# Scaling attention probabilities on GpSimd or ScalarE only, and adding FoX's causal mask in PSUM

## The chip, the cores and the metric

One core of a Trainium2 chip runs the whole program in one launch. The metric is device microseconds of one execution, and of several executions the median. The engines are TensorE (PE, with its weight loads as PEld), VectorE (DVE), ScalarE (ACT), GpSimd (POOL) and SyncE, whose queue (SP) issues every DMA.

## The reference

A decoder trunk of two residual layers over 512 tokens of width 1024, all in float32. Layer 0 mixes with DSA (kind "a": an indexer picks the top 128 keys, the rest is masked) and with FoX (kind "b": causal attention with a forgetting bias), eight heads of 64 each. Layer 1 mixes with NSA: sixteen heads, each with a compressed, a selected and a window branch that are merged by sigmoid gates. Each layer ends with a squared-ReLU MLP of width 4096. What the change touches is the softmax:

```python
def masked_softmax(s, mask):
    s = jnp.where(mask, s.astype(jnp.float32), -jnp.inf)
    m = jnp.max(s, axis=-1, keepdims=True)
    e = jnp.where(mask, jnp.exp(s - m), 0.0)
    return e / jnp.maximum(jnp.sum(e, axis=-1, keepdims=True), 1e-30)

# FoX, per block of 128 queries
logits = (q @ k.T) * scale + cum_q - cum_k            # cum: running sum of log-forget gates
p = masked_softmax(logits, key_pos <= t)
# NSA, merge
out = g0 * o_compressed + g1 * o_selected + g2 * o_window
```

## The kernel before

Every dense product is done with float32r matmuls of a high and a low part, three for one (`mm3`): weights arrive in `raw` tiles of 128x512, ScalarE (or VectorE) rounds the high part into `whi`, VectorE or GpSimd forms the low part `wlo`. In the MLP seven products of a Strassen scheme take the place of eight (`psm`).

The order of the work on each engine isn't written by hand. Generators yield operations, or lists of alternatives on different engines, and a planner (`Planner`) simulates the machine when the kernel is built: it takes the operation that can start first by its cost table (`_price`) and its latencies (`LATENCY`, `MARGIN`), breaks ties by priority (attention 10, evacuations 12, top-k 16, weights 18), and picks the alternative with the earliest end. VectorE's costs are raised by up to four times with its recent load (`BIAS`), GpSimd's and ScalarE's are not. The order is then fixed: each engine works through its list, and waits where an operand isn't there yet. Changed prices or alternatives therefore reorder the list of every engine.

Attention is done in units: one head and one block of 128 queries `qb` against n = 128 (qb + 1) keys (`unit`, line 770). A unit takes a tile `t` (four exist), forms the bias, runs two matmuls into a PSUM bank `pss` (two exist), adds the bias and takes the row extreme in one VectorE operation (`nm`), runs Exp on ScalarE with the row sum `den`, the reciprocal `rec` on VectorE, scales the probabilities by `rec` and, in NSA, by the gate (`gat`), transposes them on TensorE by the identity (`ptp`, two banks) and copies them out to `pt`, from which the products with the values are run (`po`). The scaling is one operation with two factors, on GpSimd or VectorE:

```python
        g = 1.0 if gate is None else gate
        yield [e.tensor_scalar(t[:, :n], t[:, :n], rec, g, op0=OP.mult, op1=OP.mult) for e in (G, V)]
```

There are 64 units in layer 0 (32 FoX units first, then 32 DSA units, whose bias `scr` is the finished top-k mask) and 128 in layer 1 (selected and window branch; the bias is the causal mask alone). Only a FoX unit forms its bias: `b_bias` (line 1152) adds the broadcast row of the head's cumulated gates (`bb`, two tiles, brought by a DMA) and the causal mask (`cm`, a part of the constants tile `call`) into `t`, on VectorE or GpSimd. Up to six units run beside each other (`WIN`), and between them dense matmuls of the same layer.

`ident` and `cm` lie in `call`, which comes in one DMA, issued by `load_thread` (line 456) ahead of the fifth weight tile. The identity is used by every transpose, and for the diagonal matrices `dg` in `Stats.end` (line 606), by which the row norms are turned at the start.

Of the kernel before, what the change touches and what calls it, by code (L numbers as in the profile page):

```python
# [9 lines left out]
F32R = mybir.dt.float32r  # L10
AF = mybir.ActivationFunctionType
OP = mybir.AluOpType
AX = mybir.AxisListType.X

P = 128
S = 512
# [1 line left out]
NEG = -1e30  # L18
GONE = -3e38
EPS = 1e-6  # L20
CONSTS = [("gains", 32), ("ident", 128), ("cm", 512), ("kvg", 2), ("kig", 1), ("bfg", 1), ("rowv", 1),
          ("pek", 16), ("pev", 16), ("bgate", 48), ("cmm", 128), ("w2k", 128), ("w2v", 64),
          ("fold", 62)]
CONST_AT, NCONST = {}, 0
for _n, _w in CONSTS:
    CONST_AT[_n] = (NCONST, _w)
# [21 lines left out]
PR_ATT = 10  # L48
PR_EV = 12
# [119 lines left out]
class Planner:  # L169
# [16 lines left out]
    def spawn(self, gen, prio):  # L186
        self.count += 1
        self.resume([gen, prio, 0.0, None, self.count], None)
# [8 lines left out]
    def put(self, slots, *tiles):  # L197
        for t in tiles:
            slots.free.append((self.now, self.engine))
            slots.back(t)  # L200
        self.serve()
# [76 lines left out]
    def bias(self, engine, t):  # L278
        b = BIAS.get(engine, 0)
        if not b:  # L280
            return 0
        last, load = self.load.get(engine, (0.0, 0.0))
        load *= math.exp(-max(0.0, t - last) / TAU)
        return b * max(0.0, load - FLOOR)
# [58 lines left out]
def group(ops):  # L343
    o = Op(ops[0].engine, 0.0, [], [], [])
    for x in ops:
        o.cost += x.cost
        o.calls += x.calls
        o.reads += x.reads
        o.writes += x.writes
    return o  # L350
# [3 lines left out]
def trunk(ctx: ExitStack, tc: tile.TileContext, A):  # L354
# [3 lines left out]
    def pool(name, bufs, space=bass.MemoryType.SB):  # L358
        return ctx.enter_context(tc.tile_pool(name=name, bufs=bufs, space=space))

    cp, sp, mp, few, xq = pool("cp", 1), pool("sp", 1), pool("mp", 24), pool("few", 4), pool("xq", 1)
# [6 lines left out]
    K = Slots(pool("kp", 8), "k", 8, full, F32R)  # L368
    Q = Slots(pool("qp", 8), "q", 8, full, F32R)
    TU = Slots(pool("tu", N_TU), "tu", N_TU, full)  # L370
    TE = Slots(pool("te", N_TE), "te", N_TE, full)
# [11 lines left out]
    V, SC, G, T = (Queue(n, e) for n, e in  # L383
                   (("DVE", nc.vector), ("ACT", nc.scalar), ("POOL", nc.gpsimd), ("PE", nc.tensor)))
    SY = Queue("SP", nc.sync)
    spawn, put, done = pl.spawn, pl.put, pl.set
# [4 lines left out]
    def small(n, name="sm"):  # L391
        return mp.tile([P, n], F32, tag=f"m{n}", name=name)

    def copy(out, src):
        return [SC.activation(out, src, AF.Copy), V.tensor_copy(out, src)]
# [27 lines left out]
    mhalf = cp.tile([P, 4], F32, name="mhalf")  # L423
    C = {n: call[:, o:o + w] for n, (o, w) in CONST_AT.items()}
    gains = gall.rearrange("p (a k) -> p a k", k=KT)
    ident, cm = C["ident"], C["cm"]
    cmm = C["cmm"].rearrange("p (a b) -> p a b", b=32)
    rowv, kvg, bgate = C["rowv"], C["kvg"], C["bgate"]
    bfg, kig = C["bfg"][0:8], C["kig"][0:64]
# [18 lines left out]
    def shaped(t, shape):  # L448
# [4 lines left out]
            return t[:, :n].rearrange("p (a b) -> p a b", b=shape[1])  # L453
        return t[:, :n]

    def load_thread():
        yield SY.dma_start(gall, A["consts"][:, 0:32])
        at = 0
        for j in jobs:
            if j.load is not None:  # L460
                yield from j.load()
            for i, (src, shape) in enumerate(j.chunks):
                n = shape[0] * shape[1]
                if at in X_AT:
                    for k in range(*X_AT[at]):
                        x = yield O.get("x", F32)
                        yield SY.dma_start(x, A["xT"][:, k, :])
                        done(x0[k], x)
                if at in XN_AT:
                    done(xnf[XN_AT.index(at)])  # L470
                if at == CONST_PUT:
                    yield SY.dma_start(call, A["consts"])
                at += 1
                raw = yield RAW.get("raw")
                yield SY.dma_start(raw[:, :n], src)
                done(j.raw[i], raw)
# [277 lines left out]
        return (yield ("all", [slots.get(name, dtype), slots.get(name, dtype)]))  # L754


    def scores(ps, qs, kk, qb):
        n = P * (qb + 1)
        q = qs[:, qb * P:(qb + 1) * P]
        return group([T.matmul(ps[:, :n], q, kk[0][:, :n], start=True, stop=False),  # L760
                      T.matmul(ps[:, :n], q, kk[1][:, :n], start=False, stop=True)])

    def pt_dst(pt, h, qb):
        if h == 0:
            return pt[:, 0:qb + 1, qb * P:(qb + 1) * P]
        base = pt[:, 4 - qb, 0:P]
        return bass.AP(tensor=base.tensor, offset=base.offset,
                       ap=[base.ap[0], [S + P, qb + 1], [1, P]])

    def unit(qs, kk, qb, bias, pt, h, fut, gate=None):  # L770
        n = P * (qb + 1)
        t = yield TU.get("t")
        b = yield from bias(t)
        ps = yield PSS.get("pss")
        yield scores(ps, qs, kk, qb)
        nm, den, rec = small(1, "nm"), small(1, "den"), small(1, "rec")
        yield V.tensor_tensor_reduce(out=t[:, :n], in0=ps[:, :n], in1=b, op0=OP.add, op1=OP.min,
                                     scale=-0.125, scalar=3e38, accum_out=nm)
        put(PSS, ps)
        yield SC.activation(t[:, :n], t[:, :n], AF.Exp, scale=-1.0, bias=nm, accum_out=den)  # L780
        yield V.reciprocal(rec, den)
        g = 1.0 if gate is None else gate
        yield [e.tensor_scalar(t[:, :n], t[:, :n], rec, g, op0=OP.mult, op1=OP.mult) for e in (G, V)]
        tt = yield PST.get("ptp")
        yield group([T.transpose(tt[:, j * P:(j + 1) * P], t[:, kb * P:(kb + 1) * P], ident)
                     for kb in range(qb + 1) for j in [kb if h == 0 else qb - kb]])
        put(TU, t)
        yield copy(pt_dst(pt, h, qb), tt[:, :n].rearrange("p (a b) -> p a b", b=P))
        put(PST, tt)
        done(fut)  # L790
# [138 lines left out]
    used = {h: 0 for h in range(8)}  # L929
# [220 lines left out]
    Job([], free_ckv)  # L1150

    def b_bias(bb, n):
        def g(t):
            yield [e.tensor_tensor(t[:, :n], bb[0][:, :n], cm[:, S - n:S], op=OP.add) for e in (V, G)]
            bb[1] -= 1
            if not bb[1]:
                put(B, bb[0])
            return t[:, :n]
        return g

    def plain_bias(ap):
        def g(t):
            return ap
            yield
        return g

    och = futures(8)
    ord_ = {"prev": None}
# [1 line left out]
    def attention_ab():  # L1170
        for kind in ("b", "a"):
            for i in range(4):
                q = yield qf[kind, i]
                k = yield kf[kind, i]
                pt = yield PT.get("pt")
                fs = []
                for n_ in range(8):
                    if kind == "b":
                        h, qb = n_ // 4, n_ % 4
                        if qb == 0:  # L1180
                            yield cumf[2 * i + h]
                            bt = yield B.get("bb")
                            yield SY.dma_start(bt, cumd[2 * i + h, :].partition_broadcast(P))
                            bb = [bt, 4]
                        bias = b_bias(bb, P * (qb + 1))
                    else:
                        h, qb = n_ % 2, n_ // 2
                        yield scf[qb]
                        bias = plain_bias(scr[qb])
                    fu = Future()  # L1190
                    fs.append(fu)
                    spawn(unit(q[h], k[h], qb, bias, pt, h, fu), PR_ATT)
                    if len(fs) > WIN:
                        yield fs[-WIN]
                spawn(pv_ab(kind, i, fs, pt, q, k), PR_PV)
# [673 lines left out]
    mlp(hN3, u3, st3, A["w1"][1], A["w2"][1], after1)  # L1869

    spawn(load_thread(), PR_W)
    spawn(split_thread(), PR_W)
    spawn(dense_thread(), PR_MM)
# [20 lines left out]
def _layout(i):  # L1894
    import numpy as np
    f4 = np.float32
    c = np.ascontiguousarray
    d = {}
    d["xT"] = c(i["x"][0].T.reshape(8, 128, 512).transpose(1, 0, 2))
    d["xn"] = c(i["x"][0].reshape(4, 128, 1024).transpose(1, 0, 2))  # L1900
    g = np.stack([i["attn_norm"][0], i["mlp_norm"][0], i["attn_norm"][1], i["mlp_norm"][1]])
    d["fing"] = c(i["final_norm"].reshape(2, 512))
    K = {}
# [21 lines left out]
    q, kc, vc, ks, vs, kw, vw, gl = np.split(w, np.cumsum([1024] + [128] * 6), axis=1)  # L1925
# [19 lines left out]
    tc_[0:8], tc_[8:16] = cos, cos  # L1945
    ts_[0:8], ts_[8:16] = -sin, sin
    d["tabs"] = np.stack([np.concatenate([tc_, tc_]), np.concatenate([ts_, ts_])], axis=1)
    K["ident"] = np.eye(128, dtype=f4)
    cm = np.zeros((128, 512), f4)
    cm[:, 384:] = np.where(np.arange(128)[None, :] <= np.arange(128)[:, None], 0.0, NEG)  # L1950
    K["cm"] = cm
    t = np.arange(128)[:, None, None] + 128 * np.arange(4)[None, :, None]
    n = np.arange(32)[None, None, :]
# [29 lines left out]
```

## Time and profile before

| what | value |
|---|---|
| median of 3 runs | 1252.09 us (1251.19 to 6821.25) |
| profiled execution | 1250.76 us |
| its span, first to last instruction | 1249.0 us |
| mean granted TensorE clock | 0.991 |
| busy: PE, DVE, ACT, POOL | 96%, 78%, 55%, 25% |

The span and the 1.76 us around it make the profiled execution's own time, which lies 1.33 us under the median. One of the three runs, of 6821.25 us, stands by itself; the other two are 0.9 us apart. Times in rows count from the start of the span.

### The profile page before, as it was taken

To read this page: it belongs to the slowest core of one execution; us is meant where nothing else is said; L and a number is where in the kernel's file an instruction comes from. 1 tells how busy PE (TensorE), PEld (TensorE's weight loads), DVE (VectorE), ACT (ScalarE), POOL (GpSimd) and SP (SyncE) were. 2 spreads that over 40 slices of the span, in tenths; PEclk is the share of its full clock that TensorE was granted. 3 is DMA by queue.
4 is the path that set the end of the run, shared out by engine and by line. 5 is a ranking of instruction groups with operands and counts; after the bars stand their busy time and mean duration, and the time that the engine had idled before them with its cause. 6 is when DMAs were issued, how large, how long until landed. Compare 5 with 4: busy or idle time off the path is not lost.

```text
span 1249.0 us, 18399 instructions
## 1 busy us (share of the span) xinstructions
PE 1201.6 (96%) x5894; PEld 963.6 (77%) x5894; DVE 972.7 (78%) x2097; ACT 683.5 (55%) x1492; POOL 315.8 (25%) x332
## 2 busy tenths in 40 slices
PE   6899999999999999999998899999999999999997
PEld 5688767678888888888877676677788888888885
DVE  5999967746896977968878977776469879689697
ACT  5364456645554545545556677777555454454453
POOL 0655867530000000000156655654200000000000
PEclk9799999999999999999999999999999999999999
DMA  8352545563405135053346411142252350531601
GB/s 311 87 139 81 159 121 147 153 215 112 160 25 180 66 94 176 1 169 102 106 130 173 137 51 51 52 122 95 73 161 75 93 177 1 159 111 50 193 11 68
DMA packets 79425, 143.26 MB, mean 115 GB/s; under 512 B 9880, under 2 KB 12440, under 8 KB 79328
## 3 DMA queue, kind: packets, MB, share of 16 engines
q1 hardware_dynamic: 79328, 142.08, 37.2%
q8 instruction: 47, 0.77, 0.3%
q14 instruction: 50, 0.41, 0.1%
HBM read 116.60 MB, written 8.40 MB: 100 GB/s over the span
## 4 chain that ended last, share of the span: by engine, by line
PE 83%; DVE 7%; DMA 3%; ACT 2%; issue 2%; SPq 1%; POOL 1%; POOLq 0%; DVEq 0%; ACTq 0%
PE psd L335 44%; PE psm L335 24%; PE po L335 4%; PE pss L335 4%; PE ptp L335 4%; DVE t L335 1%; PE psv L335 1%; SPq L335 1%; DMA raw<-wab 1%; PE pth L335 1%; DVE m L335 1%; DVE q L335 1%; DVE scr L335 1%; ACT t L335 1%; DVE wlo L335 1%
## 5 line engine op out<-in xcount | busy, mean ns | idle before, releaser
L335 PE MATMUL psd<-uh,whi 128*128 128x512 f32 x760 | 303.5, 399 | 8.3 <-ACT uh L335 5.5
L335 PE MATMUL psd<-ul,whi 128*128 128x512 f32 x760 | 299.8, 394 | 0.0
L335 PE MATMUL psd<-uh,wlo 128*128 128x512 f32 x760 | 299.2, 394 | 0.0
L335 ACT ACTIVATE whi<-raw 128x512 fp32r<-128x512 f32 (+2 forms) x245 | 148.0, 607 | 151.1 <-PE psd L335 100.3
L335 ACT ACTIVATE whi<-w 128x512 fp32r<-128x512 f32 x224 | 134.5, 627 | 141.3 <-PE psd L335 50.1
L335 POOL TENSOR_TENSOR wlo<-raw,whi 128x512 fp32r<-128x512 f32 (+2 forms) x82 | 106.4, 1301 | 401.9 <-DVE wlo L335 318.5
L335 PEld LDWEIGHTS psd<-uh,whi 128*128 128x128 f32 x760 | 145.0, 191 | 37.5 <-ACT uh L335 5.5
L335 PEld LDWEIGHTS psd<-uh,wlo 128*128 128x128 f32 x760 | 144.7, 190 | 31.1 <-DVE wlo L335 0.2
L335 PEld LDWEIGHTS psd<-ul,whi 128*128 128x128 f32 x760 | 145.1, 191 | 28.4 <-DVE ul L335 0.5
L335 DVE TENSOR_TENSOR wlo<-raw,whi 128x512 fp32r<-128x512 f32 (+1 forms) x170 | 121.4, 720 | 48.1 <-ACT whi L335 47.5
L335 DVE TENSOR_TENSOR wlo<-w,whi 128x512 fp32r<-128x512 f32 x224 | 147.2, 685 | 8.5 <-ACT whi L335 7.7
L335 ACT ACTIVATE t<-t,nm 128x128 f32<-128x128 f32 (+1 forms) x192 | 107.2, 560 | 46.0 <-DVE nm L335 43.9
L335 PE MATMUL psm<-whi,a 128*128 128x512 f32 x384 | 121.3, 389 | 0.0
L335 POOL TENSOR_TENSOR rn<-ms,mhalf 128x4 f32<-128x4 f32 (+1 forms) x10 | 10.4, 1042 | 381.4 <-DVE ms L335 380.5
L335 PE MATMUL psm<-whi,acts 128*128 128x512 f32 x320 | 103.8, 389 | 0.0
L335 ACT ACTIVATE pt<-ptp 128x384 f32<-128x384 f32 (+3 forms) x186 | 76.1, 434 | 31.4 <-PE ptp L335 30.8
L335 PE MATMUL psd<-whi,oh 128*128 128x512 f32 x256 | 90.1, 401 | 0.7 <-ACT oh L335 0.7
L335 PE MATMUL ptp<-call,t 128*128 128x128 f32 x480 | 79.3, 277 | 11.6 <-DVE t L335 6.1
L335 DVE TENSOR_TENSOR w<-w,w 128x512 f32<-128x512 f32 x128 | 85.9, 686 | 0.8
L335 PEld LDWEIGHTS ptp<-call,t 128*128 128x128 f32 x480 | 56.7, 140 | 36.8 <-issue 9.3
L335 DVE CUSTOM_DVE_ANT_0 t<-pss,call 128x128 f32<-128x128 f32 (+3 forms) x136 | 61.7, 471 | 29.0 <-PE pss L335 26.7
L335 PEld LDWEIGHTS psm<-whi,a 128*128 128x128 f32 x384 | 72.1, 188 | 14.9
(244 smaller groups left out, 2177.8 us busy)
## 6 DMA issues: line engine op xcount, KB each, us to landing
raw<-w SPq DMA_DIRECT2D x128, 256.0 KB, 2.8
w<-w SPq DMA_DIRECT2D x128, 256.0 KB, 4.5
raw<-wab SPq DMA_DIRECT2D x38, 256.0 KB, 3.0
raw<-wout SPq DMA_DIRECT2D x32, 256.0 KB, 2.8
raw<-wc SPq DMA_DIRECT2D x24, 256.0 KB, 3.8
raw<-wcn SPq DMA_DIRECT2D x16, 152.0 KB, 2.3
x<-xT SPq DMA_DIRECT2D x8, 256.0 KB, 6.1
xn<-xn SPq DMA_DIRECT2D x4, 512.0 KB, 7.4
```

What stands on the lines that cost most here:

```text
L335: call = lambda: getattr(self.engine, method)(*args, **kw)
```

## The change

Three edits. First, the probabilities are scaled on GpSimd or ScalarE, no longer on VectorE; where there is a gate, `rec` is multiplied by it in an operation of its own on VectorE, on one column. Second, in FoX's units the causal mask is added by a third matmul, of the identity and the mask's 128x128 block in float32r (`idr`, `cmr`), into the diagonal block of `pss`; the row `bb` is then the bias of the VectorE operation directly, and `b_bias` gives its tile back after that operation. Third, the identity leaves the constants: it comes in a DMA of its own into a borrowed `te` tile, and two ScalarE copies round it and the mask into `idr` and `cmr` (`squares`). All transposes and `dg` read `idr` as float32.

```diff
-    ident, cm = C["ident"], C["cm"]
+    idr = cp.tile([P, P], F32R, name="idr")
+    cmr = cp.tile([P, P], F32R, name="cmr")
+    ident, cm = f(idr), C["cm"]
...
+    def squares():
+        yield const
+        x = yield TE.get("id")
+        yield SY.dma_start(x[:, 0:P], A["ident"])
+        yield SC.activation(idr, x[:, 0:P], AF.Copy)
+        yield SC.activation(cmr, cm[:, S - P:S], AF.Copy)
+        put(TE, x)
...
         yield SY.dma_start(gall, A["consts"][:, 0:32])
+        spawn(squares(), PR_EV)
...
                     yield SY.dma_start(call, A["consts"])
+                    done(const)
...
-    def scores(ps, qs, kk, qb):
+    def scores(ps, qs, kk, qb, causal=False):
         n = P * (qb + 1)
         q = qs[:, qb * P:(qb + 1) * P]
-        return group([T.matmul(ps[:, :n], q, kk[0][:, :n], start=True, stop=False),
-                      T.matmul(ps[:, :n], q, kk[1][:, :n], start=False, stop=True)])
+        mask = [T.matmul(ps[:, n - P:n], idr, cmr, start=False, stop=False)] if causal else []
+        return group([T.matmul(ps[:, :n], q, kk[0][:, :n], start=True, stop=False)] + mask +
+                     [T.matmul(ps[:, :n], q, kk[1][:, :n], start=False, stop=True)])
...
-        b = yield from bias(t)
+        bias_ap, b = bias
         ps = yield PSS.get("pss")
-        yield scores(ps, qs, kk, qb)
+        yield scores(ps, qs, kk, qb, causal)
...
-        g = 1.0 if gate is None else gate
-        yield [e.tensor_scalar(t[:, :n], t[:, :n], rec, g, op0=OP.mult, op1=OP.mult) for e in (G, V)]
+        if gate is not None:
+            yield V.tensor_tensor(rec, rec, gate, op=OP.mult)
+        yield [G.tensor_scalar(t[:, :n], t[:, :n], rec, 1.0, op0=OP.mult, op1=OP.mult),
+               SC.activation(t[:, :n], t[:, :n], AF.Copy, scale=rec)]
...
     def b_bias(bb, n):
-        def g(t):
-            yield [e.tensor_tensor(t[:, :n], bb[0][:, :n], cm[:, S - n:S], op=OP.add) for e in (V, G)]
+        def used():
             bb[1] -= 1
             if not bb[1]:
                 put(B, bb[0])
-            return t[:, :n]
-        return g
+        return bb[0][:, :n], used
```

## Rows read from the trace of the kernel before

**Rows 1.** Busy us by stage: PE, PEld, DVE, ACT, POOL; clock, DMA share, GB/s.
```profile
0.00:80.00 80.00, 63.33 (x254) 49.48 (x255) 63.83 (x100) 40.68 (x68) 31.90 (x26) 0.91 0.60 189
80.00:205.00 125.00, 117.07 (x666) 93.89 (x665) 108.14 (x304) 64.77 (x161) 84.34 (x83) 1.00 0.45 124
205.00:265.00 60.00, 57.52 (x326) 43.59 (x327) 42.66 (x132) 41.15 (x114) 33.36 (x39) 1.00 0.56 154
265.00:640.00 375.00, 373.93 (x1683) 308.46 (x1680) 290.07 (x499) 188.15 (x337) 17.91 (x14) 1.00 0.37 117
695.00:892.00 197.00, 193.01 (x1169) 139.42 (x1167) 137.27 (x497) 143.43 (x428) 107.43 (x135) 1.00 0.27 80
```

**Rows 2.** Longest waits, 80 to 265 us: total, times, longest.
```profile
PE ptp L335 <- DVE t L335: 6.1, 7, 1.7
...
PE ptp L335 <- DVE rec L335: 1.5, 2, 0.9
...
PEld ptp L335 <- POOL t L335: 1.2, 3, 0.6
```

**Rows 3.** Timeline of 149 to 156 us: start, duration, instruction, idle before.
```profile
153.80 1.26 POOL L335 TENSOR_TENSOR wlo<-raw,whi 128x512 fp32r<-128x512 f32 x1
153.91 1.23 DVE L335 TENSOR_SCALAR t<-t,rec 128x128 f32<-128x128 f32 x1
...
155.29 0.30 PE L335 MATMUL ptp<-call,t 128*128 128x128 f32 x1 [1.70 <-DVE t L335]
```

**Rows 4.** The tile t, 80 to 265 us: ns min/median/max, first and last start.
```profile
L335 POOL TENSOR_SCALAR t<-t,rec x40: 371/586/1197, 93.2 to 260.0; 128x512 f32<-128x512 f32 x14, 128x384 f32<-128x384 f32 x10, 128x128 f32<-128x128 f32 x8, 128x256 f32<-128x256 f32 x8
L335 POOL TENSOR_TENSOR t<-bb,call x27: 458/1003/1427, 86.2 to 193.1; 128x384 f32<-128x384 f32 x8, 128x128 f32<-128x128 f32 x7, 128x256 f32<-128x256 f32 x6, 128x512 f32<-128x512 f32 x6
L335 DVE CUSTOM_DVE_ANT_0 t<-pss,t x32: 265/477/692, 87.0 to 196.5; 128x128 f32<-128x128 f32 x8, 128x256 f32<-128x256 f32 x8, 128x384 f32<-128x384 f32 x8, 128x512 f32<-128x512 f32 x8
L335 DVE TENSOR_SCALAR t<-t,rec x24: 285/801/1445, 89.9 to 252.0; 128x128 f32<-128x128 f32 x8, 128x256 f32<-128x256 f32 x8, 128x384 f32<-128x384 f32 x6, 128x512 f32<-128x512 f32 x2
L335 DVE TENSOR_TENSOR t<-bb,call x5: 674/694/1515, 151.2 to 183.4; 128x512 f32<-128x512 f32 x2, 128x256 f32<-128x256 f32 x2, 128x128 f32<-128x128 f32 x1
```

**Rows 5.** By shape, ACT, 695 to 892 us: busy, mean ns | idle before.
```profile
L335 ACT ACTIVATE t<-t,nm 128x512 f32<-128x512 f32 x32 | 23.0, 720 | 8.6 <-DVE nm L335 8.4
...
L335 ACT ACTIVATE t<-t,nm 128x128 f32<-128x128 f32 x32 | 12.6, 397 | 2.1 <-DVE nm L335 2.1
```

**Rows 6.** Chain of work that ended last, 80 to 205 us: shares.
```profile
by line: PE psd L335 32.1%; PE psv L335 10.2%; issue 8.6%; DVE t L335 8.5%; SPq L335 6.1%; DVE scr L335 5.4%; PE ptp L335 5.3%; POOL t L335 3.8%; PE pss L335 3.7%; PE po L335 3.7%; DMA raw<-wab 2.7%; DMA raw<-wuk 2.5%; POOL q L335 1.4%; DVE
```

**Rows 7.** Waits of the DMA queue, 80 to 265 us.
```profile
SPq L335 <- POOL wlo L335: 58.2, 23, 5.9
```

**Rows 8.** Timeline of 86 to 92 us, PE.
```profile
86.31 0.34 PE L335 MATMUL pss<-bk,bq 128*128 128x128 f32 x2
...
86.48 0.33 PE L335 MATMUL psv<-whi,uh 128*128 128x256 f32 x1
```

**Rows 9.** The chain in order of time, 138 to 205 us, one piece.
```profile
174.13 0.44 PE ptp L335 x4
```

**Rows 10.** The tile t, 695 to 892 us.
```profile
L335 POOL TENSOR_SCALAR t<-t,rec,gat x100: 443/660/1517, 696.8 to 885.6; 128x384 f32<-128x384 f32 x31, 128x512 f32<-128x512 f32 x25, 128x256 f32<-128x256 f32 x24, 128x128 f32<-128x128 f32 x20
L335 DVE TENSOR_SCALAR t<-t,rec,gat x28: 335/777/1676, 697.9 to 863.4; 128x128 f32<-128x128 f32 x12, 128x256 f32<-128x256 f32 x8, 128x512 f32<-128x512 f32 x7, 128x384 f32<-128x384 f32 x1
```

**Rows 11.** Instructions by shape, DVE, the whole span.
```profile
L335 DVE TENSOR_TENSOR ms<-parts 128x1 f32<-128x1 f32 x4 | 0.6, 160 | 1.0 <-ACT sq L335 1.0
```

**Rows 12.** Longest waits, 695 to 892 us.
```profile
PEld ptp L335 <- POOL t L335: 3.5, 7, 0.9
...
PE ptp L335 <- DVE rec L335: 1.6, 2, 1.2
```

**Rows 13.** Timeline of the start, 0 to 34 us.
```profile
9.67 0.33 SPq L335 DMA_DIRECT2D call<-consts  x1
...
15.01 1.06 ACT L335 ACTIVATE xn<-xn 128x1024 f32<-128x1024 f32 x1 [0.65 <-DMA xn<-xn]
```

More of the change, by code (lines that the diff above doesn't have):

```diff
@@ L20 @@
 EPS = 1e-6
-CONSTS = [("gains", 32), ("ident", 128), ("cm", 512), ("kvg", 2), ("kig", 1), ("bfg", 1), ("rowv", 1),
+CONSTS = [("gains", 32), ("cm", 512), ("kvg", 2), ("kig", 1), ("bfg", 1), ("rowv", 1),
           ("pek", 16), ("pev", 16), ("bgate", 48), ("cmm", 128), ("w2k", 128), ("w2v", 64),
@@ L454, in shaped @@
         return t[:, :n]
+    const = Future()
+    def squares():
[5 more added lines that the diff above has]
+        put(TE, x)
     def load_thread():
         yield SY.dma_start(gall, A["consts"][:, 0:32])
+        spawn(squares(), PR_EV)
         at = 0
@@ L768, in pt_dst, with unit @@
                        ap=[base.ap[0], [S + P, qb + 1], [1, P]])
-    def unit(qs, kk, qb, bias, pt, h, fut, gate=None):
+    def unit(qs, kk, qb, bias, pt, h, fut, gate=None, causal=False):
         n = P * (qb + 1)
         t = yield TU.get("t")
-        b = yield from bias(t)
+        bias_ap, b = bias
         ps = yield PSS.get("pss")
-        yield scores(ps, qs, kk, qb)
+        yield scores(ps, qs, kk, qb, causal)
         nm, den, rec = small(1, "nm"), small(1, "den"), small(1, "rec")
-        yield V.tensor_tensor_reduce(out=t[:, :n], in0=ps[:, :n], in1=b, op0=OP.add, op1=OP.min,
+        yield V.tensor_tensor_reduce(out=t[:, :n], in0=ps[:, :n], in1=bias_ap, op0=OP.add, op1=OP.min,
                                      scale=-0.125, scalar=3e38, accum_out=nm)
         put(PSS, ps)
+        b()
         yield SC.activation(t[:, :n], t[:, :n], AF.Exp, scale=-1.0, bias=nm, accum_out=den)
         yield V.reciprocal(rec, den)
-        g = 1.0 if gate is None else gate
-        yield [e.tensor_scalar(t[:, :n], t[:, :n], rec, g, op0=OP.mult, op1=OP.mult) for e in (G, V)]
+        if gate is not None:
+            yield V.tensor_tensor(rec, rec, gate, op=OP.mult)
+        yield [G.tensor_scalar(t[:, :n], t[:, :n], rec, 1.0, op0=OP.mult, op1=OP.mult),
+               SC.activation(t[:, :n], t[:, :n], AF.Copy, scale=rec)]
         tt = yield PST.get("ptp")
@@ L1157, in g @@
                 put(B, bb[0])
-            return t[:, :n]
-        return g
+        return bb[0][:, :n], used
     def plain_bias(ap):
[L1162 to L1165, printed above, removed]
+        return ap, lambda: None
     och = futures(8)
@@ L1191, in attention_ab @@
                     fs.append(fu)
-                    spawn(unit(q[h], k[h], qb, bias, pt, h, fu), PR_ATT)
+                    spawn(unit(q[h], k[h], qb, bias, pt, h, fu, causal=kind == "b"), PR_ATT)
                     if len(fs) > WIN:
@@ L1947, in _layout @@
     d["tabs"] = np.stack([np.concatenate([tc_, tc_]), np.concatenate([ts_, ts_])], axis=1)
-    K["ident"] = np.eye(128, dtype=f4)
+    d["ident"] = np.eye(128, dtype=f4)
     cm = np.zeros((128, 512), f4)
```

## The prediction

> **What bounds the kernel now.** I read the busy times by stage first [rows 1]. TensorE is the bound: in the MLP of layer 0 (265 to 640 us) it is busy for 373.9 of 375 us, and the MLP of layer 1 does the same work. The change touches no operation there. What it can move lies in the two attention stages: 80 to 265 us (FoX, then DSA) and 695 to 892 us (NSA). There TensorE is idle for 125 - 117.1 + 60 - 57.5 = 10.4 us and for 197 - 193.0 = 4.0 us. A busy matmul row also covers its pipelined tail, so some idle time hides under it; still, the attention stages hold little to win, 14 us as shown and perhaps twice that.
>
> Then the waits inside the first stage [rows 2]. TensorE waits 6.1 us in seven places for `t` from VectorE ahead of a transpose, and 1.5 and 1.2 us for `rec` and for `t` from GpSimd. One of the seven shows what they are [rows 3]: a scaling of 128x128 on VectorE starts at 153.91 just behind a GpSimd operation that started at 153.80, lasts 1.23 us, ends when that one does, and TensorE idles 1.70 us for it. The same instruction needs 285 ns at best, and the median of all 24 is 801 [rows 4]. So VectorE's scaling is slow because GpSimd works beside it, and it stands in the way of VectorE's own queue.
>
> **Removed in the first stage.** VectorE loses 24 scalings and 5 bias sums: by the medians 24 x 0.80 + 5 x 0.69 = 22.7 us, of 108.1 + 42.7 busy. GpSimd loses 27 bias sums at 1.00 us, 27 us of 84.3 [rows 1, 4]. Scalings now go to GpSimd or ScalarE. A ScalarE copy with a scale per row isn't in the trace on these shapes; its nearest rows are the Exps of the same tile, which read one value per row as well: 397 to 720 ns over four shapes, 0.56 us in the middle (first and last in [rows 5]), against 371 to 1197 on GpSimd. ScalarE's price I take as those rows; below them it could fall by what Exp costs more than a copy, which no row of these shapes shows.
>
> For the seven waits this means: a scaling of 1.2 to 1.5 us becomes one of 0.4 to 0.7. Seven times 0.8 is 5.6; I count **-5.5 us** of the 8.8 us in [rows 2]. Bounds: all of them, -8.8, or none, where ScalarE's queue of Exps and evictions holds the scaling back as long as GpSimd did. What is late next is `rec` itself, behind Exp and VectorE's reduction.
>
> GpSimd's freed time has a second use. The DMA queue waits 58.2 us for low parts (`wlo`) that GpSimd makes, because a weight tile can't be loaded until its slot is free [rows 7], and the queue's own steps are 6.1% and landings of `raw` 5.2% of the chain from 80 to 205 us [rows 6], 14 us. A third less work on GpSimd lets some of this go; I take **-2.5 us**, between 0 (the planner fills GpSimd with other alternatives, since VectorE's costs are raised by its load) and -7, half of it.
>
> **Added in the first stage.** 32 mask matmuls, one in each FoX unit. Two score matmuls of 128 columns take 86.48 - 86.31 = 0.17 us, 0.085 each [rows 8]; a transpose of 128 columns takes 0.11 [rows 9]; half of a score matmul's slot is the other end, 0.045. So 32 x 0.085 = **+2.7 us**, bounds 1.4 and 3.5. I count it in full, as TensorE is 94% busy there. The bias tile `bb` is now held until the VectorE reduction and not until the sum. Its next load stands in SP's queue, with weight loads and the moves of q and k behind it; two tiles are there and a head's four units use one, so I cost this at nothing; if the cover goes, it is one reduction, 0.7 us at most [rows 4], for each of six loads. `t` now waits for no sum, which gives nothing, since the sum was early.
>
> **NSA.** VectorE loses 28 scalings (777 ns, 21.8 us) and gets 128 products of one column. No such product lies in a unit; the nearest row is a 128x1 sum of 160 ns [rows 10, 11], so 20.5 us of VectorE's time at most; the other end is nothing, as VectorE idles 60 us in this stage [rows 1]. I take the row: VectorE's load stays as it was. Each unit's path gets 0.16 us longer ahead of the scaling, and 0.1 us shorter where ScalarE (0.40 to 0.72) takes it from GpSimd (0.44 at best, median 0.66). Behind the product on VectorE stand the reductions of the next units; ahead of it nothing new. TensorE's waits that come from the scaling are 3.5 us (weight loads, on `t` from GpSimd) and 1.6 us (`rec`) [rows 12]. Gain and loss are of one size here: **0 us**, bounds -5.1 and the ScalarE rival below.
>
> **The start.** SP issues one more DMA right behind the constants, 0.33 us [rows 13], ahead of weight loads and of `xn`; the bytes are the same in sum. ScalarE gets two copies of 128x128 that wait for it; behind them stand the squares of `xn`, the first at 15.01 us, and these feed the norms and through them all evacuations. **+0.3 us**; 1 us if the identity lands late. The identity is wanted by the `dg` products only after the norms, over 10 us later, which hides the rest.
>
> **Sum**: -5.5 - 2.5 + 2.7 + 0 + 0.3 = -5.0 us on the profiled execution's 1250.76 us: 1245.8. The median stands 1.33 us above that execution, so I forecast **1247 us**.
>
> **A rule against the change.** In this trace VectorE isn't the quick engine for the scaling: 801 and 777 ns in the median [rows 4, 10], ScalarE's rows of the same shapes 397 to 720 [rows 5]. The Trainium skill, page "ScalarE: Activation LUTs", section "Rules for kernel authors", says to use VectorE and not ScalarE for a multiplication. The trace agrees only for VectorE undisturbed, 285 ns for 128x128; by that rule the seven waits would not shrink and the sum would be +0.5 us, a case of the second rival below. The Trainium skill's page "SBUF — State Buffer" says, under "Who interferes with whom", that a VectorE `tensor_scalar` and GpSimd can contend for a shared port that one of them holds for its whole instruction; [rows 3] agree, and this is why I don't follow the first rule here.
>
> **Rivals.**
> - *ScalarE becomes the bound of NSA (slower).* ScalarE is busy 143.4 of 197 us there [rows 1]. All 128 scalings on it would be 128 x 0.56 = 71.7 us [rows 5]: 215 us, 18 more than the stage lasts. From about (197 - 143.4) / 0.56 = 96 of 128 scalings on, Exps and evictions queue behind scalings, and TensorE waits. For it: a scaling is cheap on ScalarE, and the planner takes the earliest end, without a load factor on ScalarE. Against it: a filled ScalarE makes GpSimd's end the earlier one in the planner's own count, and GpSimd has 90 us free. Price: 18 us and the first stage's -5.0: 1264 by the profiled execution, **1265**.
> - *The waits are only replaced (slightly slower).* Every order is drawn anew, GpSimd fills with `wlo`, and transposes wait for ScalarE as they did for VectorE. Then only the additions stay: +2.7 + 0.3, and 1.6 in NSA, if 0.16 us falls on ten transposes that were waiting: **1257**. For it: the seven waits are as much queue as duration, and TensorE's price is certain. Against it: 27 us of work vanish from GpSimd, and no engine but TensorE gets as much.
> - *More comes free (faster).* The full bounds of gain: -8.8 - 7 - 5.1, with 1.4 + 0.3 added: -19.2, **1233**. For it: VectorE is busy 108 of 125 us from 80 to 205 us [rows 1] and is relieved there, and idle time hides under pipelined matmuls. Against it: the chain of 80 to 205 us goes over many other links (top-k scores, moves, weight loads), none of which the change touches.
> - *The change doesn't do what it says:* ScalarE gets next to no scalings and all go to GpSimd, which would have 128 x 0.66 = 84 us of them in NSA, 18 more than now, in the 90 us it has free. The time would be that of the second rival.
>
> **How the numbers follow.** The forecast (1240 to 1252 by itself) 0.50; waits replaced 0.24; ScalarE the bound 0.13; more free 0.13. The range takes in the second rival, most of the third and, of the first, the cases in which the planner stops short of filling ScalarE: 1237 to 1262. A measurement of this kernel can tell about 2% (25 us) from no change. Faster by that means 1227, below even the third rival: 0.02. Slower means 1277, beyond the first rival, unless the start loses the clock as well (it is 0.91 of full speed from 0 to 80 us now): 0.03. So 0.95 for within.
>
> **What the changed profile would show.** No `TENSOR_SCALAR` of `t` on VectorE; 32 more `pss` matmuls of 128 columns, `idr` with `cmr`, within 0.05 to 0.11 us of their neighbours; TensorE's wait for `t` in 80 to 265 us near 1 us and not 6; more than half of the 192 scalings on ScalarE, which in NSA is then near 175 of 197 us busy (55 to 90 scalings at 0.56 less what overlaps); 128 one-column products; GpSimd with a fifth less work before 265 us; the FoX and DSA stages shorter by some 5 us, NSA as long as now. The prediction is wrong if NSA takes over 203 us, if GpSimd's `wlo` is as late as before, or if the start shifts by more than 2 us: a different order of loads or a lower granted clock there would show it.

## The result, and the profile after

The changed kernel takes 1262.5 us in the median (1261.3 to 1263.45 in four runs), against 1251.8 for the kernel before beside it: a ratio of 1.0084, interval 1.0067 to 1.0102. It is slower by some 10.5 us, where 5 us less were forecast. Its profiled execution took 1261.3 us, with a span of 1259.5.

Where the time went is read first from one form of matmul that only the MLPs have. The view is that of the tile `psm`; after the count stand the shortest, median and longest ns, then the first and last start. Each kernel has one row for the MLP of layer 0 and one for that of layer 1. Before:

```profile
L335 PE MATMUL psm<-whi,a x192: 389/389/476, 343.1 to 628.2; 128*128 128x512 f32 x192
L335 PE MATMUL psm<-whi,a x192: 388/389/389, 956.5 to 1239.9; 128*128 128x512 f32 x192
```

After:

```profile
L335 PE MATMUL psm<-whi,a x192: 389/389/476, 337.8 to 623.0; 128*128 128x512 f32 x192
L335 PE MATMUL psm<-whi,a x192: 388/389/389, 967.0 to 1250.3; 128*128 128x512 f32 x192
```

The first MLP starts 5.3 us earlier, and lasts as long as before. From its last such matmul to the first of layer 1, the stretch that holds NSA, it was 956.5 - 628.2 = 328.3 us and is now 967.0 - 623.0 = 344.0: 15.7 us more. The second MLP is unchanged. So the first stage came out as forecast in sum, and the whole loss lies in NSA, for which the forecast was nothing. Below, this stretch is called the NSA stretch and is taken the same way from each kernel's two rows. It is read from one profiled execution of each kernel, so it stands beside the ratios and does not replace them.

Busy time by stage, after, with the columns of [rows 1]. The stages are cut where this kernel's lie:

```profile
80.00:205.00 125.00, 122.73 (x719) 101.34 (x718) 96.34 (x295) 72.33 (x182) 60.94 (x60) 1.00 0.45 124
205.00:260.00 55.00, 54.42 (x308) 41.97 (x308) 38.04 (x121) 42.91 (x120) 24.80 (x24) 1.00 0.61 171
...
690.00:903.00 213.00, 196.45 (x1173) 140.14 (x1173) 153.71 (x616) 173.40 (x487) 75.33 (x89) 1.00 0.24 73
```

From 80 to 260 us TensorE idles 2.9 us, where it was 10.4 from 80 to 265. In NSA it idles 16.6 us, where it was 4.0. VectorE's busy time there rose from 137.3 to 153.7 us, though it has lost its scalings; ScalarE's rose from 143.4 to 173.4.

TensorE's longest waits in the first stage, 80 to 260 us, which answer to [rows 2], and in NSA, 690 to 903 us, which answer to [rows 12]:

```profile
PEld ptp L335 <- ACT t L335: 2.5, 6, 0.8
...
PE ptp L335 <- ACT t L335: 0.7, 2, 0.4
...
PEld ptp L335 <- ACT t L335: 15.0, 21, 1.8
...
PE ptp L335 <- ACT t L335: 7.9, 9, 1.7
```

The first two lines are the first stage: the transposes themselves wait 0.7 us for `t` in place of 6.1, their weight loads 2.5. The others are NSA. Taken alone they accuse ScalarE: the transposes wait for a `t` that it has scaled. What ScalarE itself waited for is in the chain of work that ended last, 690 to 903 us:

```profile
by line: PE psd L335 19.2%; PE po L335 12.7%; PE ptp L335 11.9%; PE pss L335 10.3%; ACT t L335 8.6%; DVE rec L335 8.0%; DVE t L335 6.4%; issue 3.7%; DVE q L335 3.3%; DVE whi L335 2.4%; DVE wlo L335 2.3%; ACT pt L335 1.7%; PE psc L335 1.4%; 
```

`rec` on VectorE holds 8.0% of 213 us, 17 us. In NSA two operations write it, the reciprocal (20.3 us in all, 159 ns each) and the new product. By shape, with busy time and mean ns:

```profile
L335 DVE TENSOR_TENSOR rec<-rec,gat 128x1 f32<-128x1 f32 x128 | 37.5, 293 | 2.7
```

The product of one column costs 293 ns in the mean, against 160 in the row on which I priced it [rows 11]. The tile's view gives its spread:

```profile
L335 DVE TENSOR_TENSOR rec<-rec,gat x128: 96/159/1249, 692.2 to 892.5; 128x1 f32<-128x1 f32 x128
```

The median is as priced, the longest eight times that. Of the single instructions in the trace 31 last over 200 ns, 22.4 us together, and each of the 31 ends within 0.02 us behind the end of a GpSimd instruction: 27 times an operation of 512 columns with two operands from tiles, four times a scaling of `t`. Not every product beside GpSimd is held: 18 of the other 97 overlap one of its instructions too and stay under 200 ns. One of the 31, with what follows, in the timeline from 806 to 809 us:

```profile
806.67 1.27 POOL L335 TENSOR_TENSOR q<-q,cs 128x512 f32<-128x512 f32 x1 [4.58 <-DVE rec L335]
807.13 0.82 DVE L335 TENSOR_TENSOR rec<-rec,gat 128x1 f32<-128x1 f32 x1
...
807.88 0.68 DVE L335 CUSTOM_DVE_ANT_0 t<-pss,call 128x512 f32<-128x512 f32 x1
...
808.05 0.62 ACT L335 ACTIVATE t<-t,rec 128x384 f32<-128x384 f32 x1 [0.22 <-DVE rec L335]
...
808.72 0.55 PE L335 MATMUL ptp<-idr,t 128*128 128x128 f32 x3 [1.68 <-ACT t L335]
```

GpSimd's product ends at 807.94, VectorE's single column at 807.95. Then come the scaling, and TensorE after 1.68 us of idling; the next unit's reduction, which stands behind the product in VectorE's queue, starts only at 807.88. It is what [rows 3] show, in another place: there a scaling of 128x128 lasted as long as the GpSimd operation beside it, here a product of one column does.

### The profile page after: what moved, and what is told of

Same layout as the page of the kernel before. It is cut to its first block, busy times and chain, and to the rows that moved or that the text cites. A ratio compares the mean times of both kernels' runs of the same rounds, so it can differ in the third digit from the quotient of the medians.

```text
span 1259.5 us, 18473 instructions
## 1 busy us (share of the span) xinstructions
PE 1206.7 (96%) x5926; PEld 969.6 (77%) x5926; DVE 971.1 (77%) x2192; ACT 722.4 (57%) x1578; POOL 251.7 (20%) x249
## 4 chain that ended last, share of the span: by engine, by line
PE 80%; DVE 10%; ACT 4%; DMA 3%; issue 2%; POOL 0%; SPq 0%; DVEq 0%; POOLq 0%; ACTq 0%
PE psd L335 42%; PE psm L335 24%; PE po L335 3%; PE ptp L335 3%; PE pss L335 3%; ACT t L335 2%; DVE rec L335 1%; DVE t L335 1%; PE psv L335 1%; DMA raw<-wab 1%; DVE m L335 1%; DVE q L335 1%; DVE wlo L335 1%; DVE scr L335 1%; PE pth L335 1%
## 5 line engine op out<-in xcount | busy, mean ns | idle before, releaser
L335 ACT ACTIVATE whi<-raw 128x512 fp32r<-128x512 f32 (+2 forms) x233 | 140.9, 609 | 156.2 <-PE psd L335 107.3
L335 POOL TENSOR_TENSOR wlo<-raw,whi 128x512 fp32r<-128x512 f32 (+2 forms) x86 | 110.6, 1289 | 435.7 <-DVE wlo L335 318.6
L335 PE MATMUL ptp<-idr,t 128*128 128x128 f32 x480 | 80.3, 278 | 13.9 <-ACT t L335 8.6
L335 PEld LDWEIGHTS ptp<-idr,t 128*128 128x128 f32 x480 | 56.8, 140 | 39.4 <-ACT t L335 17.5
L335 POOL TENSOR_TENSOR rn<-ms,mhalf 128x4 f32<-128x4 f32 (+1 forms) x10 | 10.4, 1044 | 382.0 <-DVE ms L335 381.1
L335 DVE TENSOR_TENSOR hN<-psm,hN 128x512 f32<-128x512 f32 x112 | 74.0, 685 | 2.9 <-PE psm L335 2.6
```

The source lines that it names most:

```text
L335: call = lambda: getattr(self.engine, method)(*args, **kw)
```

## The experiments

Three theories stood. **A**: the product, which lies between Exp and scaling in every NSA unit and can be held up by GpSimd. **B**: ScalarE, which got 80 of the 128 scalings. **C**: the new order that the planner drew. Each ratio is to the kernel before, run beside it on the same chip. The intervals are about 0.2% wide to either side, 2 to 3 us.

**Layer 1 scaled as before.** The product goes, and both factors stand in one operation again. The last line's calls are shortened by dots; it is that of the changed kernel.

```diff
+        if gate is not None:
+            yield [e.tensor_scalar(t[:, :n], t[:, :n], rec, gate, op0=OP.mult, op1=OP.mult) for e in (G, V)]
+        else:
             yield [G.tensor_scalar(...rec, 1.0...), SC.activation(...scale=rec)]
```

> Layer 1 scales its probabilities as the kernel before did (GpSimd or VectorE, both factors in one operation, no product of rec and gate); layer 0 and the mask matmul stay as changed. Both theories put the whole loss into NSA, so both expect the gain of the first stage to stand alone: median 1244 to 1249 us, NSA from its first unit to the last product with the values again about 197 us instead of 213. If it stays above 1255, the loss isn't in the scaling of layer 1, and both theories fall.

Measured: 1245.13 us, ratio 0.9952 (0.9928 to 0.9976). The NSA stretch is 327.6 us. The loss lies in the scaling of layer 1 and nowhere else.

**No product.** The two lines of the product are taken out.

> As changed, but the product of rec and gate is left out, so the gates of the selected and window branches aren't applied. Theory A (the one-column product on VectorE, which lies between Exp and scaling and lasts up to 1.25 us while GpSimd works) expects NSA back at 195 to 200 us and a median of 1244 to 1250. Theory B (ScalarE's queue, which 80 of 128 scalings fill) expects nearly no change, 1258 to 1263, since ScalarE keeps Exps, evictions and scalings. Between 1251 and 1257 both hold a part.

Measured: 1248.42 us, 0.9971 (0.9958 to 0.9985); NSA stretch 329.5 us, with 76 scalings on ScalarE. This is A's number; B had wanted 1258 or more. The planner drew a new order here, so C is still open.

**Product, but no ScalarE.** In layer 1 the scaling after the product is on GpSimd or VectorE.

> As changed, but in layer 1 the scaling after the product is on GpSimd or VectorE, none on ScalarE. Theory A expects the loss to stay, 1258 to 1268, as the product is still on every unit's path and VectorE has the scalings again. Theory B expects it gone, 1245 to 1252.

Measured: 1258.78 us, 1.0062 (1.0044 to 1.008); NSA stretch 343.8 us. The loss stays without ScalarE. These two runs are a pair: with ScalarE and no product it goes, with the product and no ScalarE it stays.

**The product with one operand from a tile.** All engines have the order of the changed kernel; only this instruction's form is another.

```diff
-            yield V.tensor_tensor(rec, rec, gate, op=OP.mult)
+            yield V.tensor_scalar(rec, rec, gate, None, op0=OP.mult)
```

> As changed, but the product is a tensor_scalar: one operand from a tile, the gate as the per-row scalar. The planner draws the same order for TensorE. Theory A, in its form that the product waits for GpSimd (31 of 128 lasted over 0.2 us, 22.4 us together), expects those long ones gone and 5 to 12 us back: 1250 to 1257. If the product costs by its place and not by its duration, or by theory B, 1260 to 1264.

Measured: 1254.98 us, 1.0013 (0.9996 to 1.0029). The tile's view of this kernel:

```profile
L335 DVE TENSOR_SCALAR rec<-rec,gat x128: 119/213/219, 692.3 to 886.4; 128x1 f32<-128x1 f32 x128
```

None is held up any more, the longest being 219 ns, though 35 of the 128 begin and end inside a GpSimd operation. By the ratios (1.0084 - 1.0013) x 1252 = 8.9 us came back, with some 3 us to either side from the two intervals, though an undisturbed product is 54 ns slower in this form. In the profiled execution the NSA stretch is 340.1 us, only 3.9 less than in the changed kernel. That execution was the slowest of the ten, 1257.47 us, and its granted clock fell at the end of NSA. The stretch from 850 to 905 us, with the columns of [rows 1], first of this kernel and then of the changed one:

```profile
850.00:905.00 55.00, 51.34 (x264) 35.90 (x263) 29.75 (x117) 37.73 (x107) 8.63 (x13) 0.88 0.23 73
...
850.00:905.00 55.00, 50.46 (x300) 35.88 (x299) 31.39 (x138) 41.63 (x118) 9.49 (x16) 1.00 0.25 82
```

A granted clock of 0.88 in the mean is a part of the stretch at the lower level, 1.2 GHz; before it TensorE had been busy for 153.4 of 160 us, and why the clock fell no run shows. Four of the ten executions had a mean clock of 0.982 to 0.986 and took 1255.8 to 1257.5 us; the other six, at 0.988 to 0.992, took 1249.9 to 1255.2. So the waits for GpSimd are about half of the 16.4 us that the next run gives the product, or somewhat more, since the lower clock lies in this kernel's time as well.

**The product planned, but not issued.** Here the order is that of the changed kernel again, to the last instruction, without the 128 products; the gates are left out.

```diff
+            ghost = V.tensor_tensor(rec, rec, gate, op=OP.mult)
+            ghost.calls = []
+            yield ghost
```

> As changed, with the order of every engine as the planner drew it with the product in it, but the 128 products are not issued (the gates aren't applied). Nothing is drawn anew, so what changes is the product's own time on the chip. Theory A (the product, by its place and by its waits for GpSimd) expects 9 to 14 us back, 1248 to 1253. If the loss came from the order that the planner drew around the product's price, or from ScalarE, it stays at 1258 to 1263.

Measured: 1247.58 us, 0.9953 (0.9935 to 0.997); NSA stretch 332.2 us. That is (1.0084 - 0.9953) x 1252 = 16.4 us for the product alone, its time, its waits and its place in the path, again with some 3 us to either side; A had expected 9 to 14. Theory C falls for the loss: the same order is fast without it. So does B, and the row of busy times says how clearly (691 to 891 us, with 80 scalings on ScalarE):

```profile
691.00:891.00 200.00, 193.70 (x1172) 141.22 (x1172) 124.93 (x488) 172.10 (x489) 77.02 (x89) 0.99 0.27 79
```

ScalarE is busy 172.1 of 200 us, as long as in the changed kernel and in less time, and TensorE loses no more than 6.3 us.

**The product twice.** The order is the same once more; behind each product stands a second one, by ones.

```diff
+            twice = V.tensor_tensor(rec, rec, gate, op=OP.mult)
+            twice.calls += V.tensor_tensor(rec, rec, ones[:, 0:1], op=OP.mult).calls
```

> As changed, with each of the 128 products followed by a second one of the same kind, rec times a column of ones, in the same order of all engines (the planner counts both as one). Theory A (time and waits of a one-column product with two operands from tiles, between Exp and scaling) expects half to all of the first one's 15 us once more: 1269 to 1278. If only the first product's place matters and not its time, 1261 to 1266.

Measured: 1276.26 us, 1.0192 (1.0168 to 1.0217); NSA stretch 358.2 us. The second costs (1.0192 - 1.0084) x 1252 = 13.5 us, after 16.4 for the first. With none, one and two products in one order of work, the time goes 0.9953, 1.0084, 1.0192.

**GpSimd alone in layer 1**, with both factors in one operation.

> As changed, but layer 1 scales on GpSimd alone, with both factors in one operation: no product, no ScalarE, no VectorE. Theory A expects no loss against the version that scales layer 1 as before: 1243 to 1249. If GpSimd alone is too slow for 128 scalings (84 us of 0.66 each in some 197), 1252 to 1260. By theory B, with ScalarE free, also 1243 to 1249: this run asks only whether an alternative is needed at all.

Measured: 1247.38 us, 0.9955 (0.994 to 0.997). One engine was enough for all 128 scalings, and neither ScalarE nor VectorE was needed for them.

**The parts of layer 0.** First the mask and the identity's load with all scalings as before, then the kernel before with only the scalings of layer 0 changed.

> The mask matmul, the bias without sums and the identity's own load, as changed; all scalings as before, on GpSimd or VectorE with both factors. If the gain of the first stage came from the bias sums that GpSimd loses (27 us), 1245 to 1248; if it came from the scalings that VectorE loses there, 1250 to 1255, since the 32 matmuls (2.7 us) stay.

> The kernel before, with the scalings of layer 0 on GpSimd or ScalarE; layer 1, the bias sums and the identity's load as before. If the scalings that VectorE loses make the gain of the first stage, 1242 to 1247; if the bias sums do, 1250 to 1253.

Measured: 1247.59 us, 0.9957 (0.994 to 0.9973), and 1247.33 us, 0.9951 (0.9936 to 0.9966). Each alone brings about what both bring together (0.9952). The expectations had set them against each other, and the first run has the number for which the bias sums make the gain, the second lies 0.3 us above the range for which the scalings make it: they are no alternatives. The view of `t` of the first, 80 to 265 us:

```profile
L335 POOL TENSOR_SCALAR t<-t,rec x46: 371/586/1647, 88.1 to 254.5; 128x512 f32<-128x512 f32 x14, 128x256 f32<-128x256 f32 x13, 128x384 f32<-128x384 f32 x12, 128x128 f32<-128x128 f32 x7
...
L335 DVE TENSOR_SCALAR t<-t,rec x18: 282/472/1271, 91.9 to 246.5; 128x128 f32<-128x128 f32 x9, 128x384 f32<-128x384 f32 x4, 128x256 f32<-128x256 f32 x3, 128x512 f32<-128x512 f32 x2
```

Without bias sums GpSimd takes 46 scalings in place of 40, and the 18 that stay on VectorE last 472 ns in the median and not 801; in my reading because less of GpSimd's work lies beside them, which no run takes apart. TensorE's transposes, which waited 6.1 us for `t` from VectorE before [rows 2], wait 0.2 us for it in the first run, and in the second not at all for VectorE, but 2.9 us for ScalarE. So the two edits cure one and the same wait, by either of the engines that made it.

**A new order alone.** One of the planner's latencies is raised by 10 ns (213 for 203), first in the kernel before, then in the version that scales layer 1 as before.

> The kernel before, with one of the planner's latencies 10 ns higher (VectorE to GpSimd, 213 for 203), so that the order is drawn anew with nothing else changed. It shows what a new order alone moves: within 3 us of the kernel before if the gain of 5 to 7 us in the first stage is the edits' own; at 1246 to 1248 if any new order would have brought it.

> The version that scales layer 1 as before, with the same 10 ns: 1243 to 1249 if its gain is the edits' own, up to 1253 if it is the luck of one order.

Measured: 1252.82 us, 1.0009 (0.9998 to 1.0019), and 1247.55 us, 0.9955 (0.9938 to 0.9973). One new draw of each moved either kernel by less than 3 us, so the gain of some 5 us in the first stage is hardly the luck of one order.

## Why the prediction was wrong

**The step that failed** is the one on NSA: "the nearest row is a 128x1 sum of 160 ns", "20.5 us of VectorE's time at most", and from there "Gain and loss are of one size here". The duration was taken from a row outside the attention, and it was made an upper bound. The row was of four sums; none stood beside a wide GpSimd operation. Two ran inside one of a single column, and were not held. One of them, in the kernel before:

```profile
1236.16 0.55 POOL L335 TENSOR_TENSOR rn<-ms,mhalf 128x1 f32<-128x1 f32 x1 [321.75 <-DVE ms L335]
...
1236.41 0.16 DVE L335 TENSOR_TENSOR ms<-parts 128x1 f32<-128x1 f32 x1 [0.33 <-ACT sq L335]
```

I had the very row that speaks against the bound: [rows 3] show a VectorE operation held by GpSimd to its end, and I used that to explain what the change removes, and not to price what it adds. With 31 of 128 held, the products took 37.5 us of VectorE and not 20.5. What they cost the kernel was 16.4 us and not nothing: each stands between Exp and scaling, and TensorE's idle time in NSA rose from 4.0 to 16.6 us, so other work covered little of the longer path. The duration is not the whole of the miss. In the form that is never held the product still leaves some 7.5 us, (1.0013 - 0.9953) x 1252, so setting the gain against the loss to 0 was wrong for an undisturbed product as well. NSA took 213 us, over the 203 that the prediction named as a sign of being wrong.

The Trainium skill has a rule for such holds, on the page "SBUF — State Buffer", section "Who interferes with whom": a VectorE instruction with two operands from SBUF contends with a GpSimd instruction that reads SBUF. The trace agrees for the 31 products of up to 1249 ns, not for every overlap: the 18 others stayed under 200 ns, and the two sums above were not held. The form with a single tile operand never exceeded 219 ns. The rule that I weighed and set aside, in the Trainium skill on the page "ScalarE: Activation LUTs", section "Rules for kernel authors", that a multiplication belongs on VectorE and not on ScalarE, would have been of no help. ScalarE's 80 scalings cost nothing that can be measured (0.9953 with them and without products, 0.9952 with neither), and the harm came from VectorE's multiplication.

**The first stage** came out right in sum, -5.3 us at the start of the first MLP. Its terms:
- *The waits for `t`* (-5.5 us): the 8.8 us of [rows 2] became 3.4, 0.7 of the transposes and 2.7 of their weight loads, as said. That VectorE's scalings alone were the cause was too narrow, as the run with the mask alone shows.
- *GpSimd's low parts* (-2.5 us): not so. The DMA queue's wait for them is unchanged, 58.2 us before [rows 7] and 58.6 us now, from 80 to 260 us.
- *The mask matmuls* (+2.7 us): 24 of the 32 took 57 to 62 ns to the next matmul's start, below the 85 I took and within the bounds; seven took 111 to 115, and one 445. Together that is 2.7 us, as forecast, though not spread as I had it.
- *The bias tile* (nothing, as covered): the cover failed in one place, where a reduction waited 3.57 us for the landing of `bb`, five times the 0.7 us that I had as the price of a failure:

```profile
159.49 0.29 DVE L335 CUSTOM_DVE_ANT_0 t<-pss,bb 128x128 f32<-128x128 f32 x1 [3.57 <-DMA bb<-cumd]
```

- *The start* (+0.3 us): ScalarE did wait for the identity, 2.28 us, and the first square of `xn` came at 17.58 us instead of 15.01 [rows 13]. FoX's first mask matmul starts at 86.0 us, where the first FoX scores before were at 86.31 [rows 8]; nothing is left of it there.

```profile
17.16 0.31 ACT L335 ACTIVATE idr<-id 128x128 fp32r<-128x128 f32 x1 [2.28 <-DMA id<-ident]
```

**The rivals.** 1262.5 lies near the time of the ScalarE rival, 1265, but for another reason: ScalarE got 80 scalings, fewer than the 96 from which that rival decides, was as full as I had written (173 us for 175), and the run without products shows that this costs little. None of the rivals had the product held up. What stays open is how the 7.5 us divide that remain with the form that is never held: between the product's own 213 ns in each unit, VectorE's queue behind it, and the lower granted clock in some of that kernel's executions.

**A better version** is the one that scales layer 1 as before and keeps the rest of the change, 0.9952 to the kernel before. The mask alone, the scalings of layer 0 alone and GpSimd alone in layer 1 lie within its interval.

## What to carry to other kernels

An operation that a change adds to a path is priced with its neighbours running: a duration from another place, with other work beside it, is not an upper bound, and if the trace shows one engine holding another anywhere, the same hold belongs in the price of what is added. One column was not small here, with two tile operands beside a busy GpSimd; the gate as a second factor inside the scaling that has to run anyway was cheaper by 16.5 us, (1.0084 - 0.9952) x 1252. To tell an instruction's own cost from that of a new order, plan it and don't issue it, then issue it twice.

## What the runs showed of the hardware

A product of 128x1 on VectorE with two operands from tiles took 96 to 1249 ns; the 31 of 128 that lasted over 200 ns ended within 0.02 us behind a GpSimd operation, and 18 others overlapped one and stayed under 200 ns. As `tensor_scalar`, with the gate as the scalar operand, it took 119 to 219 ns, also in the 35 cases inside a GpSimd operation. A float32r matmul of 128 columns let the next one start after 57 to 62 ns in 24 of 32 cases, although its weight load alone lasts 187 to 192 ns.
